# A fused linear layer with a low-rank term: unrolled programs over six tiles become loops over one ring, and chunks double in size

## The chip, the cores and the metric

The kernel runs on one core of a Trainium2 chip. The metric is device microseconds per execution. Three runs of the kernel before gave 165.13, 165.41 and 165.42 us, so the median is 165.41 us. All times inside an execution come from one profiled execution, counted from its first instruction.

## The reference

`x` has 16 × 2048 = 32768 rows of 256 float32 values. `W` is 256 × 256; the low-rank factors have rank 16.

```python
y = x_flat @ W
lora_out = x_flat @ lora_A
lora_out = lora_out * lora_E
lora_out = lora_out @ lora_B
y = y + scale * lora_out
```

The input is 33.5 MB, the output is as large, and the weights are small. Since everything is linear, the kernel builds one effective weight `weff = W + scale * A diag(E) B` once and multiplies every row by it.

## The kernel before, in words

**Chunks.** The rows are cut into nine chunks by `PLAN`, in units of 128 rows: 16, seven times 32, and 16. Below, "a 32-row chunk" means 32 rows on each of the 128 partitions, 4 MB; in memory each partition's share is one contiguous piece of 32 KB (16 KB for the short chunks). A chunk is loaded into one of six tiles `xy`, worked on in place, and stored from the same tile. Chunks 6, 7 and 8 reuse the tiles of chunks 0, 1 and 2.

**Steps.** A step is four rows per partition (`Q = 4`), so a 32-row chunk has 8 steps and the whole kernel 64. In a step VectorE (DVE) casts four rows to bf16 into `xb` (L146); TensorE (PE) makes eight 128×128 transposes of them into PSUM tile `ps_xt` (L176); DVE copies these to `xt` (L155); PE makes eight products with `weff` into `ps_y` (L184); ScalarE (ACT) copies the result over the input rows in `xy` (L163). `xb`, `xt`, `ps_xt` and `ps_y` have two buffers each.

**Order on the engines.** The order is written out by hand, with semaphores. DVE and ACT have all 64 steps unrolled. DVE casts step k+1 before it copies the transposes of step k. PE runs a loop of two steps with its work shifted by one step: it transposes step k+1 before it multiplies step k, so that the DVE copy of step k lies beside transposes of k+1. PE waits with `take`, an instruction that waits for a semaphore and lowers it by one (L170); DVE and ACT have their waits attached to the work instruction.

**Transfers.** All big transfers are issued by SyncE (SP) on one queue, which its 16 DMA engines work off in order. SP issues W and the loads of chunks 0 to 5 at once (L104, L102), then for each chunk waits until ACT has finished it (`s_rdy`, an ACT drain per chunk) and issues its store (L109). After the store of chunk 2 it issues the loads of chunks 6, 7 and 8, each after a wait until the store of the tile's former chunk has landed (`s_out`).

Of the kernel before, what the change touches and what calls it, by code (L numbers as in the profile page):

```python
# [6 lines left out]

PLAN = [16] + [32] * 7 + [16]  # L10

ROWS, SLOTS = 32, 6

LEAD = 6
AFTER = {2: [6, 7, 8]}

Q = 4


@with_exitstack  # L20
def kernel(
    ctx: ExitStack,
    tc: tile.TileContext,
    x: bass.AP,
    W: bass.AP,
    lora_A: bass.AP,
    lora_B: bass.AP,
    lora_E: bass.AP,
    scale: bass.AP,
    out: bass.AP,  # L30
):
    nc = tc.nc
    P = 128
    FP32 = mybir.dt.float32
    BF16 = mybir.dt.bfloat16

    x_flat = x.flatten_outer_dims()
    out_flat = out.flatten_outer_dims()
    N, K = x_flat.shape
    M = out_flat.shape[1]  # L40
    R = lora_B.shape[0]
    KC = K // P
    CHUNKS = len(PLAN)
    assert K == M and sum(PLAN) * P == N and all(b % Q == 0 for b in PLAN)

    def sbuf(name, shape, dt):
        return ctx.enter_context(nc.sbuf_tensor(name, shape, dt))

    def psum(name, shape, dt):
        return ctx.enter_context(nc.psum_tensor(name, shape, dt))  # L50

    xy = [sbuf(f"xy{s}", [P, ROWS, K], FP32) for s in range(SLOTS)]
    xb = [sbuf(f"xb{s}", [P, Q, K], BF16) for s in range(2)]
    xt = [sbuf(f"xt{s}", [P, Q, KC, P], BF16) for s in range(2)]
    w_sb = sbuf("w_sb", [P, KC, M], FP32)
    a_sb = sbuf("a_sb", [P, KC, R], FP32)
    b_sb = sbuf("b_sb", [R, M], FP32)
    e_sb = sbuf("e_sb", [R, 1], FP32)
    b_bf = sbuf("b_bf", [R, M], BF16)
    ate = sbuf("ate", [R, KC, P], BF16)  # L60
    weff = sbuf("weff", [P, KC, M], BF16)
    ident = sbuf("ident", [P, P], FP32)
    ident_bf = sbuf("ident_bf", [P, P], BF16)

    ps_xt = [psum(f"ps_xt{s}", [P, Q, KC, P], BF16) for s in range(2)]
    ps_y = [psum(f"ps_y{s}", [P, Q, M], FP32) for s in range(2)]
    ps_at = psum("ps_at", [P, KC, P], FP32)
    ps_aeb = psum("ps_aeb", [P, KC, M], FP32)

    sem = tc.alloc_semaphore  # L70
    s_w, s_a, s_b, s_e = sem("s_w"), sem("s_a"), sem("s_b"), sem("s_e")
    s_in = [sem(f"s_in{i}") for i in range(CHUNKS)]

    again = CHUNKS - SLOTS
    s_out = [sem(f"s_out{i}") for i in range(again + 1)]
    s_id = sem("s_id")
    s_lora = sem("s_lora")
    s_lpe = sem("s_lpe")
    s_xb = sem("s_xb")
    s_t = sem("s_t")  # L80
    s_xt = sem("s_xt")
    s_p = sem("s_p")
    s_y = sem("s_y")
    s_rdy = sem("s_rdy")

    starts = [sum(PLAN[:i]) * P for i in range(CHUNKS)]

    def rows_of(flat, i):
        b, r0 = PLAN[i], starts[i]
        return flat[r0:r0 + b * P, :].rearrange("(p b) k -> p b k", b=b)  # L90


    steps = [(i, r) for i, b in enumerate(PLAN) for r in range(0, b, Q)]
    n = len(steps)
    assert n % 2 == 0

    with tc.tile_critical(sync_engine=mybir.EngineType.SP, no_gpsimd_drain=True):  # L97
        sp, pe, dve, act, pool = nc.sync, nc.tensor, nc.vector, nc.scalar, nc.gpsimd


        def load(i):
            sp.dma_start(out=xy[i % SLOTS][:, :PLAN[i], :], in_=rows_of(x_flat, i)).then_inc(s_in[i], 16)  # L102

        sp.dma_start(out=w_sb[:], in_=W.rearrange("(c p) m -> p c m", p=P)).then_inc(s_w, 16)  # L104
        for i in range(LEAD):
            load(i)
        for i in range(CHUNKS):
            sp.wait_ge(s_rdy, i + 1)
            sp.dma_start(out=rows_of(out_flat, i), in_=xy[i % SLOTS][:, :PLAN[i], :]).then_inc(s_out[min(i, again)], 16)  # L109
            for later in AFTER.get(i, []):  # L110
                if later >= SLOTS:
                    sp.wait_ge(s_out[later - SLOTS], 16)
                load(later)
        for i in range(len(s_out) - 1):
            sp.wait_ge(s_out[i], 16)


        pool.memset(ident[:], 0.0).then_inc(s_id, 1)  # L118
        pool.wait_ge(s_id, 1)
        pool.affine_select(  # L120
            out=ident[:], in_=ident[:], compare_op=mybir.AluOpType.not_equal, fill=1.0,
            base=0, pattern=[[-1, P]], channel_multiplier=1,
        ).then_inc(s_id, 1)


        dve.wait_ge(s_id, 2)
        dve.tensor_copy(out=ident_bf[:], in_=ident[:]).then_inc(s_lora, 1)  # L127
        dve.wait_ge(s_b, 16)
        dve.tensor_copy(out=b_bf[:], in_=b_sb[:]).then_inc(s_lora, 1)  # L129
        dve.wait_ge(s_e, 16)  # L130
        dve.wait_ge(s_lpe, 1)
        dve.tensor_scalar(  # L132
            out=ate[:], in0=ps_at[:R, :, :], scalar1=e_sb[:], scalar2=float(scale),
            op0=mybir.AluOpType.mult, op1=mybir.AluOpType.mult,
        ).then_inc(s_lora, 1)
        dve.wait_ge(s_w, 16)
        dve.wait_ge(s_lpe, 2)
        dve.tensor_add(out=weff[:], in0=w_sb[:], in1=ps_aeb[:]).then_inc(s_lora, 1)  # L138

        def round_step(k):  # L140
            i, r = steps[k]
            if r == 0:
                dve.wait_ge(s_in[i], 16)
            if k >= 2:
                dve.wait_ge(s_t, k - 1)
            dve.tensor_copy(out=xb[k % 2][:], in_=xy[i % SLOTS][:, r:r + Q, :]).then_inc(s_xb, 1)  # L146

        round_step(0)
        for k in range(n):
            if k + 1 < n:  # L150
                round_step(k + 1)
            dve.wait_ge(s_t, k + 1)
            if k >= 2:
                dve.wait_ge(s_p, k - 1)
            dve.tensor_copy(out=xt[k % 2][:], in_=ps_xt[k % 2][:]).then_inc(s_xt, 1)  # L155


        act.dma_start(out=a_sb[:], in_=lora_A.rearrange("(c p) r -> p c r", p=P)).then_inc(s_a, 16)
        act.dma_start(out=b_sb[:], in_=lora_B).then_inc(s_b, 16)
        act.dma_start(out=e_sb[:], in_=lora_E[:, None]).then_inc(s_e, 16)  # L160
        for k, (i, r) in enumerate(steps):
            act.wait_ge(s_p, k + 1)
            act.copy(out=xy[i % SLOTS][:, r:r + Q, :], in_=ps_y[k % 2][:]).then_inc(s_y, 1)  # L163
            if r + Q == PLAN[i]:
                act.drain().then_inc(s_rdy, 1)

        def take(s):
            pe.wait_ge(s, 1).then_inc(s, -1)  # L170

        def transposes(k):
            take(s_xb)
            for j in range(Q):
                for c in range(KC):
                    t = pe.transpose(ps_xt[k % 2][:, j, c, :], xb[k % 2][:, j, c * P:(c + 1) * P], ident_bf[:])  # L176
            t.then_inc(s_t, 1)

        def products(k):
            take(s_xt)  # L180
            take(s_y)
            for j in range(Q):
                for c in range(KC):
                    m = pe.matmul(  # L184
                        ps_y[k % 2][:, j, :], xt[k % 2][:, j, c, :], weff[:, c, :],
                        start=(c == 0), stop=(c == KC - 1),
                    )
            m.then_inc(s_p, 1)

        pe.sem_inc(s_y, 2)  # L190
        pe.wait_ge(s_a, 16)
        pe.wait_ge(s_id, 2)
        for c in range(KC):
            t = pe.transpose(ps_at[:R, c, :], a_sb[:, c, :], ident[:])  # L194
        t.then_inc(s_lpe, 1)
        pe.wait_ge(s_lora, 3)
        for c in range(KC):
            m = pe.matmul(ps_aeb[:, c, :], ate[:, c, :], b_bf[:], start=True, stop=True)  # L198
        m.then_inc(s_lpe, 1)
        transposes(0)  # L200
        pe.wait_ge(s_lora, 4)
        with pe.Fori(0, n // 2 - 1):
            transposes(1)
            products(0)
            transposes(0)
            products(1)
        transposes(1)
        products(0)
        products(1)


    with tc.tile_critical(sync_engine=mybir.EngineType.SP, no_gpsimd_drain=True):
        nc.sync.wait_ge(s_out[again], 16 * (CHUNKS - again))
# [34 lines left out]
```

## Time and profile before

| | |
|---|---|
| median of three runs | 165.41 us |
| profiled execution | 165.19 us |
| its span, first to last instruction | 163.4 us |
| busy: PE, DVE, ACT | 90.8, 84.1, 66.1 us |
| moved by DMA | 67.43 MB, mean 413 GB/s |
| mean granted TensorE clock | 0.831 |

The profile counts an engine as busy while its instructions run. A group of instructions is shown with its line, engine, operation, the tiles written and read, the count, the busy time, the mean duration of one and the idle time in front of it, with what ended that idle time. "SPq" is SyncE's sequencer, which issues the transfers; a wait there is the time during which the next transfer was not yet put into the queue. The row "DMA" gives the busy share of the 16 DMA engines in 40 equal slices of 4.1 us, in tenths.

### The profile page before, as it was taken

The page shows a single profiled execution, that of the slowest core. Times are in us where ns is not written, and L with a number is a line of the kernel's source. Part 1 is how long each engine was busy: PE and PEld are TensorE (multiplying, and loading weights), DVE is VectorE, ACT ScalarE, POOL GpSimd, SP SyncE. Part 2 cuts the span into 40 slices and gives each one's busy share as a digit, 9 for nine tenths or more (in the row PEclk, how much of TensorE's full clock was granted, in tenths as well). Part 3 has the DMA queues.
Part 4 walks back from the last instruction along what each step waited for, and adds up shares of the span by engine and source line. Part 5 has one row for each costly group of instructions (what it writes and reads, how often), then busy time and mean ns, then how long its engine had stood idle before and what let it go on. Part 6 is the DMA issues. An engine that isn't in the chain of part 4 may idle for free. (4 is left out here: it accounts for less than half of the span.)

```text
span 163.4 us, 2684 instructions
## 1 busy us (share of the span) xinstructions
PE 90.8 (56%) x1028; PEld 81.6 (50%) x1028; DVE 84.1 (51%) x132; ACT 66.1 (40%) x65; POOL 0.7 (0%) x6
## 2 busy tenths in 40 slices
PE   0169499999999999990000099999992000000000
PEld 0047389999999999980000089999981000000000
DVE  0165299999999999950000169999970000000000
ACT  3002447777777777772000026777774000000000
POOL 1000000000000000000000000000000000000000
PEclk9999999999999999999555559999999755555555
DMA  4999999899999999999999998999999999999990
GB/s 133 421 433 489 393 449 449 385 473 425 403 481 393 385 409 481 393 457 425 433 433 425 441 441 383 465 437 425 425 435 433 441 409 465 417 425 441 409 409 32
DMA packets 3203, 67.43 MB, mean 413 GB/s; under 512 B 624, under 2 KB 896, under 8 KB 896
## 3 DMA queue, kind: packets, MB, share of 16 engines
q1 hardware_dynamic: 2864, 67.37, 96.4%
q10 hardware_dynamic: 336, 0.03, 0.3%
q14 instruction: 3, 0.02, 0.0%
HBM read 33.85 MB, written 33.55 MB: 412 GB/s over the span
## 5 line engine op out<-in xcount | busy, mean ns | idle before, releaser
L163 ACT COPY xy<-ps_y 128x1024 f32<-128x1024 f32 x64 | 64.8, 1013 | 56.2 <-PE ps_y L184 56.2
L184 PE MATMUL ps_y<-weff,xt 128*128 128x256 bf16 x512 | 68.6, 278 | 0.5 <-PEq L170 0.3
L146 DVE CAST xb<-xy 128x1024 bf16<-128x1024 f32 x64 | 43.6, 683 | 24.9 <-DMA xy<-in_x_dram 24.9
L176 PE MATMUL ps_xt<-ident_bf,xb 128*128 128x128 bf16 x512 | 40.9, 226 | 24.7 <-PEq L170 24.7
L184 PEld LDWEIGHTS ps_y<-weff,xt 128*128 128x128 bf16 x512 | 48.4, 100 | 6.4 <-issue 1.1
L176 PEld LDWEIGHTS ps_xt<-ident_bf,xb 128*128 128x128 bf16 x512 | 35.5, 102 | 27.3 <-issue 25.7
L155 DVE COPY xt<-ps_xt 128x1024 bf16<-128x1024 bf16 x64 | 44.2, 691 | 5.4 <-PE ps_xt L176 3.7
L194 PE MATMUL ps_at<-ident,a_sb 128*16 128x128 f32 x2 | 0.6, 402 | 4.1 <-DMA a_sb<-in_lora_A_dram 4.1
L198 PE MATMUL ps_aeb<-b_bf,ate 16*128 16x256 bf16 x2 | 0.6, 404 | 3.6 <-DVE ate L132 3.6
L129 DVE CAST b_bf<-b_sb 16x256 bf16<-16x256 f32 x1 | 0.3, 280 | 3.9 <-DMA b_sb<-in_lora_B_dram 3.9
L163 ACT ACT_TABLE_LOAD x1 | 1.3, 1283 | 2.5 <-issue 2.5
L198 PEld LDWEIGHTS ps_aeb<-b_bf,ate 16*128 16x128 bf16 x2 | 0.1, 106 | 4.1 <-DVE ate L132 4.1
L194 PEld LDWEIGHTS ps_at<-ident,a_sb 128*16 128x16 f32 x2 | 0.1, 94 | 4.1 <-DMA a_sb<-in_lora_A_dram 4.1
L132 DVE TENSOR_SCALAR ate<-ps_at,e_sb 16x256 bf16<-16x256 f32 x1 | 0.5, 472 | 1.6 <-DMA e_sb<-in_lora_E_dram 1.6
L127 DVE CAST ident_bf<-ident 128x128 bf16<-128x128 f32 x1 | 0.2, 227 | 1.7 <-POOL ident L120 1.7
L138 DVE TENSOR_TENSOR weff<-w_sb,ps_aeb 128x512 bf16<-128x512 f32 x1 | 0.7, 687 | 0.8 <-PE ps_aeb L198 0.8
L120 POOL TENSOR_SCALAR_AFFINE_SELECT ident<-ident 128x128 f32<-128x128 f32 x1 | 0.3, 293 | 0.2 <-POOL ident L118 0.2
L118 POOL MEMSET ident<- 128x128 f32 x1 | 0.2, 204 | 0.5 <-SPq L97 0.5
L229 POOL MEMSET const-bfloat16-1.0<- 128x1 bf16 x1 | 0.1, 101 | 0.0
L229 POOL MEMSET const-uint8-127<- 128x1 uint8 x1 | 0.1, 101 | 0.0
L229 POOL MEMSET const-float32-0.0<- 128x1 f32 x1 | 0.1, 98 | 0.2 <-issue 0.2
L229 POOL MEMSET const-float32-1.0<- 128x1 f32 x1 | 0.1, 98 | 0.0
## 6 DMA issues: line engine op xcount, KB each, us to landing
xy<-in_x_dram SPq DMA_DIRECT2D x7, 4096.0 KB, 29.1
out_dram<-xy SPq DMA_DIRECT2D x7, 4096.0 KB, 39.5
xy<-in_x_dram SPq DMA_DIRECT2D x2, 2048.0 KB, 16.3
out_dram<-xy SPq DMA_DIRECT2D x2, 2048.0 KB, 39.3
w_sb<-in_W_dram SPq DMA_DIRECT2D x1, 256.0 KB, 2.9
a_sb<-in_lora_A_dram ACTq DMA_DIRECT2D x1, 16.0 KB, 3.1
b_sb<-in_lora_B_dram ACTq DMA_DIRECT2D x1, 16.0 KB, 4.4
e_sb<-in_lora_E_dram ACTq DMA_DIRECT2D x1, 0.1 KB, 5.7
```

Of the source, the lines that this page charges most:

```text
L120: pool.affine_select(out=ident[:], in_=ident[:], compare_op=mybir.AluOpType.not_equal, fill=1.0, base=0, pattern=[[-1, P]], channel_multip ...
L129: dve.tensor_copy(out=b_bf[:], in_=b_sb[:]).then_inc(s_lora, 1)
L132: dve.tensor_scalar(out=ate[:], in0=ps_at[:R, :, :], scalar1=e_sb[:], scalar2=float(scale), op0=mybir.AluOpType.mult, op1=mybir.AluOpType. ...
L138: dve.tensor_add(out=weff[:], in0=w_sb[:], in1=ps_aeb[:]).then_inc(s_lora, 1)
L146: dve.tensor_copy(out=xb[k % 2][:], in_=xy[i % SLOTS][:, r:r + Q, :]).then_inc(s_xb, 1)
L155: dve.tensor_copy(out=xt[k % 2][:], in_=ps_xt[k % 2][:]).then_inc(s_xt, 1)
L163: act.copy(out=xy[i % SLOTS][:, r:r + Q, :], in_=ps_y[k % 2][:]).then_inc(s_y, 1)
L176: t = pe.transpose(ps_xt[k % 2][:, j, c, :], xb[k % 2][:, j, c * P:(c + 1) * P], ident_bf[:])
L184: m = pe.matmul(ps_y[k % 2][:, j, :], xt[k % 2][:, j, c, :], weff[:, c, :], start=(c == 0), stop=(c == KC - 1),)
L194: t = pe.transpose(ps_at[:R, c, :], a_sb[:, c, :], ident[:])
L198: m = pe.matmul(ps_aeb[:, c, :], ate[:, c, :], b_bf[:], start=True, stop=True)
L229: nc = _bacc.Bacc("TRN2", target_bir_lowering=False, num_devices=1)
```

## The change

`PLAN` becomes three chunks of 64 rows (8 MB, pieces of 64 KB) and two of 32. The six tiles become one tile `xy` of 192 rows, used as a ring: chunks 0, 1 and 2 fill it, and chunks 3 and 4 go into the two halves of chunk 0's place. SP issues three loads at the start, then the stores of chunks 0 and 1, and then, once store 0 has landed, the loads of chunks 3 and 4, and the remaining stores.

DVE and ACT no longer have unrolled programs but two loops each, a first pass over the ring of 24 turns and a second of 8. A turn is eight rows per partition, two steps. The address of a turn's rows in the ring is computed from the loop's counter. PE's loop now has 32 turns, and the shift by one step is gone: in a turn it transposes both steps and then multiplies both. DVE makes both casts and then both copies. The waits on DVE and ACT become `take` instructions. ACT drains and raises `s_rdy` in every turn. GpSimd (POOL) waits for each load and raises the semaphore `s_ld` by the number of turns that it holds; DVE takes one per turn.

In the built program each DVE and ACT loop body has an instruction for register arithmetic in front of each copy that uses the ring's address. In the body of ACT's first loop there also stands, between the first such instruction and the first copy, the load of the activation table; in the program before it stands once, ahead of the 64 copies. In ACT's second loop there is none.

```diff
-PLAN = [16] + [32] * 7 + [16]
-ROWS, SLOTS = 32, 6
-LEAD = 6
-AFTER = {2: [6, 7, 8]}
+PLAN = [64, 64, 64, 32, 32]
+RING = 192
+LEAD = 3
+AFTER = {1: [3, 4]}
 Q = 4
+TURN = 2 * Q
...
-    xy = [sbuf(f"xy{s}", [P, ROWS, K], FP32) for s in range(SLOTS)]
+    xy = sbuf("xy", [P, RING, K], FP32)
+    xy_turns = xy[:].rearrange("p (t k q) d -> p t k (q d)", k=2, q=Q)
...
         for i in range(CHUNKS):
-            sp.wait_ge(s_rdy, i + 1)
-            sp.dma_start(out=rows_of(out_flat, i), in_=xy[i % SLOTS][:, :PLAN[i], :]).then_inc(s_out[min(i, again)], 16)
+            sp.wait_ge(s_rdy, (starts[i] + PLAN[i]) // TURN)
+            sp.dma_start(out=rows_of(out_flat, i), in_=ring_of(i)).then_inc(s_out[min(i, again)], 16)
             for later in AFTER.get(i, []):
-                if later >= SLOTS:
-                    sp.wait_ge(s_out[later - SLOTS], 16)
+                sp.wait_ge(s_out[owner[later]], 16)
                 load(later)
...
+        for i in range(CHUNKS):
+            pool.wait_ge(s_in[i], 16).then_inc(s_ld, PLAN[i] // TURN)
...
-        round_step(0)
-        for k in range(n):
-            if k + 1 < n:
-                round_step(k + 1)
-            dve.wait_ge(s_t, k + 1)
-            if k >= 2:
-                dve.wait_ge(s_p, k - 1)
-            dve.tensor_copy(out=xt[k % 2][:], in_=ps_xt[k % 2][:]).then_inc(s_xt, 1)
+        for rows in passes:
+            with dve.Fori(0, rows // TURN) as turn:
+                take(dve, s_ld)
+                for k in range(2):
+                    dve.tensor_copy(out=xb[k][:], in_=xy_turns[:, bass.ds(turn, 1), k, :]).then_inc(s_xb, 1)
+                for k in range(2):
+                    take(dve, s_t)
+                    dve.tensor_copy(out=xt[k][:], in_=ps_xt[k][:]).then_inc(s_xt, 1)
...
-        for k, (i, r) in enumerate(steps):
-            act.wait_ge(s_p, k + 1)
-            act.copy(out=xy[i % SLOTS][:, r:r + Q, :], in_=ps_y[k % 2][:]).then_inc(s_y, 1)
-            if r + Q == PLAN[i]:
+        for rows in passes:
+            with act.Fori(0, rows // TURN) as turn:
+                for k in range(2):
+                    take(act, s_p)
+                    act.copy(out=xy_turns[:, bass.ds(turn, 1), k, :], in_=ps_y[k][:]).then_inc(s_y, 1)
                 act.drain().then_inc(s_rdy, 1)
...
-        transposes(0)
         pe.wait_ge(s_lora, 4)
-        with pe.Fori(0, n // 2 - 1):
+        with pe.Fori(0, turns):
+            transposes(0)
             transposes(1)
             products(0)
-            transposes(0)
             products(1)
-        transposes(1)
-        products(0)
-        products(1)
```

## The prediction

> **What bounds the kernel now.** I read the page's slices first, then the queue table, then the waits of SP.
>
> ```profile
> DMA  4999999899999999999999998999999999999990
> ...
> q1 hardware_dynamic: 2864, 67.37, 96.4%
> ...
> q14 instruction: 3, 0.02, 0.0%
> ```
>
> The DMA engines are full from the second slice to the last but one, and one queue carries nearly all of it. PE, DVE and ACT are busy for 56, 51 and 40% of the span. The transfers set the end, and compute counts only where it holds back a transfer. Next, where SP's queue waited, and how the chunks come through it:
>
> ```profile
> SPq L109 <- ACTq L165: 77.6, 7, 18.4
> SPq L102 <- DMA out_dram<-xy: 38.5, 3, 19.8
> SPq L243 <- DMA out_dram<-xy: 36.2, 1, 36.2
> ```
>
> ```profile
> 64.30 0.34 SPq L102 DMA_DIRECT2D xy<-in_x_dram  x1
> ```
>
> ```profile
> 73.99 0.34 SPq L102 DMA_DIRECT2D xy<-in_x_dram  x1
> ```
>
> ```profile
> 83.67 0.33 SPq L102 DMA_DIRECT2D xy<-in_x_dram  x1
> ```
>
> Loads 6, 7 and 8 go out when stores 0, 1 and 2 have landed; the distance of two landings, 9.68 us, is the time of 4 MB. SP waited for ACT 77.6 us in all without one idle DMA slice, since six loads (58 us) lay in the queue. The last store was issued long before its turn: the end is a 36.2 us wait for the queue. The third view is one compute step, warm (19 to 22 us) and after an idle spell (93 to 97 us):
>
> ```profile
> 19.26 0.69 DVE L146 CAST xb<-xy 128x1024 bf16<-128x1024 f32 x1 [3.37 <-DMA xy<-in_x_dram]
> ...
> 20.10 0.61 PE L176 MATMUL ps_xt<-ident_bf,xb 128*128 128x128 bf16 x8 [2.34 <-PEq L170]
> ...
> 20.85 1.03 PE L184 MATMUL ps_y<-weff,xt 128*128 128x256 bf16 x8
> ```
>
> ```profile
> 94.22 1.01 PE L176 MATMUL ps_xt<-ident_bf,xb 128*128 128x128 bf16 x8 [20.86 <-PEq L170]
> ...
> 95.03 1.91 PE L184 MATMUL ps_y<-weff,xt 128*128 128x256 bf16 x8
> ```
>
> ```profile
> L163 ACT COPY xy<-ps_y 128x1024 f32<-128x1024 f32 x64 | 64.8, 1013 | 56.2 <-PE ps_y L184 56.2
> ...
> L163 ACT ACT_TABLE_LOAD x1 | 1.3, 1283 | 2.5 <-issue 2.5
> ```
>
> Steady ACT copies start 1.32 us apart: 2.64 us for two steps, PE's own pace (0.45 us of transposes and 0.87 us of products a step, without a gap).
>
> **What the new order demands.** The bytes are the same. The packet records show 1213 ns for 32 KB and 611 ns for 16 KB, so a larger piece saves some 6 ns; a 64-row chunk takes 19.3 us, and all chunks 6 × 19.3 + 4 × 9.68 = 154.7 us against 155.0 us before. That is 0.3 us. The first chunk's packets began at 3.2 to 3.6 us, but most engines got their second only at 4.4 to 4.9 us; the first 64 KB packet (2.4 us) covers this: another 0.5 us. So load 0 lands at 22.9, load 1 at 42.2, load 2 at 61.6 us, and store 0 ends at 80.9. A spell of slow packets at 54.6 to 57.5 us cost each engine about 0.6 us; I keep it: 81.5 us. Then the queue is empty unless store 1 is in it. Behind store 1 in SP's program stand loads 3 and 4 (their wait for store 0 is over by then) and all other stores. W was issued at 0.94 us and its first packet ran at 2.03, so SP must issue store 1 by 80.4 us: 16 turns of compute have to be done by then. Before, this cover was six small loads; now it is three loads and one store.
>
> **When compute starts.** Before, data landed at 9.15 us and the first cast ran at 9.57: 0.4 us. POOL's relay (nothing is queued behind its five waits) and the address instruction add 0.2 to 0.3 (estimate from 0.05 to 0.15 us per semaphore instruction in the records). First cast 23.6; PE 0.84 us later (93.38 to 94.22) at 24.4. PE is cold: transposes 1.06, DVE's `take` 0.1, copy 0.69, PE's two takes 0.30 (20.55 to 20.85), products 1.9. The first `ps_y` is ready 4.1 us later, at 28.5 us.
>
> **A turn on PE and DVE.** Without the shift, products wait for this turn's copy: transposes 0.61, `take` 0.10, copy 0.69, takes 0.30, two lots of products 1.74: 3.44 us in place of 2.64. DVE needs 4 × 0.60 us plus its loop's branch and arithmetic, which run while the last copy runs; 0.8 us of slack cover them.
>
> **A turn on ACT.** Here is the largest term. The built program has the table load inside the first loop's body, behind the wait for `ps_y`, so I expect 24 of them in place of 1. ACT cannot overlap its turns either, as the drain holds its program until the second copy is written. So: table load 1.28, copies 0.92 and 1.01 (an estimate: DVE's operations overlap by 0.08 us when they touch; no two ACT copies of this trace do), and drain end, loop arithmetic, branch, `take`, address arithmetic. ACT shows none of these in a loop; PE's loop instruction and branch take 0.28 us, a `take` 0.08 to 0.15, an unconditional branch on SP or ACT about 0.15. I take 0.5 us for all; bounds 0.25 and 0.9, the ends of those rows for five instructions. Sum 3.75 us (3.5 to 4.15), more than PE's 3.44: ACT sets the turn. PE's missing shift is then hidden behind ACT; without the table load it would be the bound. A load of the table that is already active could in principle cost nothing; the one row says 1283 ns and I take it, nothing being nearer. The Trainium skill's page "ScalarE: Activation LUTs", section "What ACT_TABLE_LOAD costs", speaks against the change more strongly: 1283 ns (as here) and a drain of about 1380 ns for every switch to another set. By it the turn would be 5.1 us and the time about 195 us; the trace has no drain at its one load and the set is not switched, so I leave it out.
>
> **Loops and instruction fetch.** Three instruction packets ran during the execution, 0.31 us each, and each held up one engine by up to 0.95 us. Shorter programs should need none in mid-run, but the stall below aligns the 16 engines anyway. The page "Runtime: NRT & Kernel Launch", section "Instruction fetch mechanics", warns that a taken branch outside the two resident pages forces a fetch; here PE's branch was taken 30 times and PE waited 0.3 us in all before L184 for its sequencer, so I add nothing.
>
> **The sum.** ACT ends turn 16 at 28.5 + 16 × 3.75 − 0.3 (arithmetic of a turn that never comes) = 88.2 us. SP issues store 1 at 88.3, the first packet runs at 89.4: the DMA engines stand for 89.4 − 81.5 = 7.9 us. From there on the queue has stores 1 to 4 and loads 3 and 4, 77.4 us, without another gap: store 2 is ready at about 118.5 and needed at 128, store 3 at 137.5 (needed 147), store 4 at 151.5 (needed 157). Spread of the 16 engines 0.3, one lagging engine 0.4 (before, two ended 1.6 us after the others; part of that was built up before the time where the stall aligns them). End of transfers 89.4 + 77.4 + 0.7 = 167.5 us. The span before ended 1.67 us after the last packet (161.73), and the execution took 165.19 − 163.4 = 1.79 us more than its span: 171.0 us, against 165.19 of the profiled execution before. The median was 0.2 us above that, less than I can resolve. Each 0.1 us of ACT's turn is 1.6 us: 3.5 to 4.15 give 167 to 177.
>
> **The rivals.** First, PE sets the turn, since the table load is not repeated or costs little. For it: copying needs no new table. Against it: the built program and the 1283 ns row. Turn 3.44; the cold start costs 1 to 2 us; turn 16 ends at 82.9, store 1 runs at 84.0, a stall of 2.5 us; end 84.0 + 77.4 + 0.7 + 3.46 = 165.6 us, between 164.8 and 167. The stall is paid for by the 0.8 us saved on packets and by the lag of the last engines, which it wipes out.
>
> Second, on the other side, faster: compute stays under the queue altogether. It decides at 80.4 us for turn 16, that is a turn of 3.29 us or less, 0.15 below my sum on PE and 0.45 below that on ACT: cheaper handovers, and no repeated load. Then no slice is empty, and the transfers end at 3.4 + 154.7 + 0.6 + 0.7 = 159.4: 162.9 us, 162.3 to 164.3.
>
> Third, much slower: ACT's arithmetic costs a microsecond instead of a tenth (turn 4.7, time 171.0 + 16 × 0.95 = 186 us), or PE never gets its full clock (cold turn 1.06 + 0.10 + 0.69 + 0.30 + 2 × 1.71 = 5.6, about 200 us). Against a cold PE: the clock stayed full in this trace through stretches of 3.4 us that were 55% and 72% busy (15.9 to 22.7 us), and a turn is 70 to 80% busy. Against slow arithmetic: no instruction of that kind in the records takes over 0.3 us.
>
> **How the numbers follow.** ACT with the table load 0.74, PE's chain 0.13, under the queue 0.07, much slower 0.06. From 165.2 to 176.0 the range takes in most of the first two. A measurement of this kernel can tell 0.2% from no change, 0.33 us. Faster: the second rival and a third of the first, 0.12; the same: 0.04; slower: 0.84.
>
> **What would show it.** Right: the row ACT_TABLE_LOAD with 24 instances near 1283 ns; ACT copies in pairs about 3.7 us apart; SP's store of chunk 1 near 88 us with a wait for ACT in front; one hole of some two slices in the DMA row after half of the span, and none before or after. A single table load, or ACT waiting for PE in every turn, makes the first rival right; no hole at all the second. Two holes, or a low granted clock between 30 and 115 us, the third.

## The result, and the profile after

The changed kernel takes 175.11 us (median of 4 runs, 174.59 to 175.47) against 165.32 us of the kernel before in 4 runs: 1.059 times as long, with a 95% interval of 1.056 to 1.062. The profiled execution took 175.18 us with a span of 173.4 us. Forecast was 171.0 us in a range of 165.2 to 176.0: a loss of 5.8 us, where 9.8 were measured.

First the slices of the page of the kernel after. The transfers are interrupted once:

```profile
PEclk9999999999999999999999999998599999975555
DMA  8979995999959999595059799598999989999890
GB/s 306 397 333 484 484 484 242 484 484 484 484 242 484 484 484 469 257 484 242 0 242 408 317 484 484 242 484 363 484 363 484 454 348 408 408 431 469 386 469 15
```

A slice is 4.3 us. The 5s before the middle, with 242 GB/s, are no gaps: a 64 KB packet lasts 2.4 us and is put into slices as a whole, and the packet records run there without a break. The hole is `242 0 242` in the middle, two slices in all. There is no second one, and the granted clock is full for the first 27 slices, up to 117 us. Next, the groups of ACT and the waits of SP's queue (total, times, longest), both of the kernel after:

```profile
L175 ACT COPY xy<-ps_y 128x1024 f32 x64 | 61.8, 1015 | 18.2 <-ACTq L139 17.9
...
L175 ACT ACT_TABLE_LOAD x24 | 30.8, 1283 | 42.2 <-ACTq L139 42.2
```

```profile
SPq L121 <- ACTq L176: 147.3, 5, 56.6
SPq L246 <- DMA out_dram<-xy: 18.0, 1, 18.0
```

24 table loads of 1283 ns stand where one stood. SP now waits for ACT 147.3 us in place of 77.6, and its last wait for the queue is 18.0 us in place of 36.2: the last store is issued with half of the former backlog in front of it. The timeline of ACT around the hole (start, duration, what ran, and the idle time before it) gives the turn:

```profile
82.49 1.28 ACT L175 ACT_TABLE_LOAD   x1 [0.54 <-ACTq L139]
83.79 1.93 ACT L175 COPY xy<-ps_y 128x1024 f32 x2
86.25 1.28 ACT L175 ACT_TABLE_LOAD   x1 [0.53 <-ACTq L139]
87.54 1.93 ACT L175 COPY xy<-ps_y 128x1024 f32 x2
90.00 1.28 ACT L175 ACT_TABLE_LOAD   x1 [0.54 <-ACTq L139]
```

A turn is 3.755 us: load 1.28, two copies 1.93, and 0.54 us in which ACT drains, does its loop's arithmetic, branches and takes its semaphore. PE in the same stretch shows who waits for whom:

```profile
82.97 1.06 PE L183 MATMUL ps_xt<-ident_bf,xb 128*128 128x128 bf16 x16
84.94 1.95 PE L191 MATMUL ps_y<-weff,xt 128*128 128x256 bf16 x16 [0.92 <-PEq L139]
```

PE stands for 0.92 us before its products. It takes there the signal of DVE's copy and that of ACT's copy, which frees the buffer of `ps_y`, and ACT's is the later one: ACT's first copy of the turn ends at 84.80 us, DVE's first at 84.42. SP's own timeline has the moment that matters. A row that covers several issues runs from the start of the first to the end of the last, so the store of chunk 1 ends the first row:

```profile
59.48 30.39 SPq L121 DMA_DIRECT2D out_dram<-xy  x2
89.92 1.41 SPq L114 DMA_DIRECT2D xy<-in_x_dram  x2
119.58 33.80 SPq L121 DMA_DIRECT2D out_dram<-xy  x3
```

By the instruction records it was issued at 89.53 us. The packet records show store 0 ending at 81.1 to 81.4 us on 15 of the 16 DMA engines and at 82.7 on one, and the first packets of store 1 at 90.37 to 90.52: those 15 stood for 9.0 to 9.4 us.

### The profile page after: what moved, and what is told of

Read it like the earlier page. It is cut to its first block, busy times and chain, and to the rows that moved or that the text cites. A ratio compares the mean times of both kernels' runs of the same rounds, so it can differ in the third digit from the quotient of the medians.

```text
span 173.4 us, 3142 instructions
## 1 busy us (share of the span) xinstructions
PE 96.5 (56%) x1028; PEld 80.5 (46%) x1028; DVE 81.8 (47%) x132; ACT 92.6 (53%) x88; POOL 0.7 (0%) x6
## 5 line engine op out<-in xcount | busy, mean ns | idle before, releaser
L191 PE MATMUL ps_y<-weff,xt 128*128 128x256 bf16 x512 | 64.6, 279 | 26.2 <-PEq L139 25.5
L175 ACT COPY xy<-ps_y 128x1024 f32 x64 | 61.8, 1015 | 18.2 <-ACTq L139 17.9
L191 PEld LDWEIGHTS ps_y<-weff,xt 128*128 128x128 bf16 x512 | 47.5, 99 | 39.9 <-issue 31.0
L165 DVE COPY xt<-ps_xt 128x1024 bf16<-128x1024 bf16 x64 | 41.4, 687 | 39.6 <-DVEq L139 39.6
L175 ACT ACT_TABLE_LOAD x24 | 30.8, 1283 | 42.2 <-ACTq L139 42.2
L162 DVE CAST xb<-xy 128x1024 bf16 x64 | 41.2, 685 | 14.3 <-DVEq L139 14.3
L183 PE MATMUL ps_xt<-ident_bf,xb 128*128 128x128 bf16 x512 | 35.6, 225 | 14.9 <-PEq L139 14.9
L183 PEld LDWEIGHTS ps_xt<-ident_bf,xb 128*128 128x128 bf16 x512 | 32.8, 101 | 16.4 <-issue 15.6
```

Of the source, the lines that this page charges most:

```text
L162: dve.tensor_copy(out=xb[k][:], in_=xy_turns[:, bass.ds(turn, 1), k, :]).then_inc(s_xb, 1)
L165: dve.tensor_copy(out=xt[k][:], in_=ps_xt[k][:]).then_inc(s_xt, 1)
L175: act.copy(out=xy_turns[:, bass.ds(turn, 1), k, :], in_=ps_y[k][:]).then_inc(s_y, 1)
L183: t = pe.transpose(ps_xt[k][:, j, c, :], xb[k][:, j, c * P:(c + 1) * P], ident_bf[:])
L191: m = pe.matmul(ps_y[k][:, j, :], xt[k][:, j, c, :], weff[:, c, :], start=(c == 0), stop=(c == KC - 1),)
```

## The experiments

The theory is the prediction's: the repeated table load makes ACT's turn 3.75 us, store 1 comes too late for the queue, and the transfers never make up the hole. The rivals are that the loss belongs to the chunks or to the loops themselves, whatever ACT does. Times are medians, and ratios are to the kernel before in the same session. All kernels start from the kernel after, and diffs are against it.

### The table load once

```diff
+    warm = sbuf("warm", [R, 1], FP32)
...
+        act.wait_ge(s_b, 16)
+        act.copy(out=warm[:], in_=b_sb[:, 0:1])
         for rows in passes:
             with act.Fori(0, rows // TURN) as turn:
```

> The changed kernel with one tiny ScalarE copy ahead of the loops, so that the table load stands there once and not in the loop. Theory (ScalarE's turn with a table load in it makes store 1 late): 1 table load in place of 24, the turn falls from 3.76 to about 3.49 us, which is what the second pass shows, store 1 is issued near 84 us in place of 89.5, and the time falls by the same 5.3 us to 168 to 170 us. A stall of 3 to 4 us is left, which belongs to the missing shift of TensorE. Rival (TensorE and VectorE without the shift set the turn anyway, and the table load lies in their shade): no change, 175 us. Rival (the stall has another cause, such as 8 MB transfers): no change either.

169.39 us, 1.024 [1.019, 1.029]. Lines of its groups, its slices and ACT's timeline:

```profile
L173 ACT ACT_TABLE_LOAD x1 | 1.3, 1283 | 2.5 <-issue 2.5
```

```profile
DMA  8699979979995996999199599989897999799990
```

```profile
78.07 1.93 ACT L178 COPY xy<-ps_y 128x1024 f32 x2 [1.57 <-ACTq L140]
81.56 1.93 ACT L178 COPY xy<-ps_y 128x1024 f32 x2 [1.56 <-ACTq L140]
```

One early copy draws the load out of the loop. The turn falls to 3.49 us, now set by the PE and DVE chain (ACT idles 1.56 us in it); store 1 goes out at 83.55, and the hole shrinks to one slice, all as the theory said. The place of the load in the loop is worth 5.7 us of the loss of 9.8 (175.11 less 169.39; 5.8 by the two ratios).

### The chunks and the ring alone

DVE and ACT are unrolled and PE has its shift by one step, as in the kernel before; `PLAN`, ring, `LEAD` and `AFTER` are those of the kernel after.

```diff
-        for rows in passes:
-            with dve.Fori(0, rows // TURN) as turn:
...
+        round_step(0)
+        for k in range(n):
+            if k + 1 < n:
+                round_step(k + 1)
...
+        for k, (i, r) in enumerate(steps):
+            act.wait_ge(s_p, k + 1)
+            act.copy(out=ring_of(i, r, Q), in_=ps_y[k % 2][:]).then_inc(s_y, 1)
```

> The ring, the plan and the transfers of the changed kernel with the unrolled programs and the shifted TensorE loop of the kernel before. Theory: a turn of two steps is 2.64 us, store 1 is ready near 70 us, the queue never runs dry, and the time is 164 to 165.5 us, a little under the kernel before, since the pieces are larger. Rival (the large chunks themselves cost the time, by the late start of compute or by slower packets): 168 us or more, with a hole in the DMA row.

165.97 us, 1.002 [1.001, 1.003]: level with the kernel before, and above what was expected. Store 1 was issued at 70.89 us; the slices have no hole, and the row for instruction packets has the three of the kernel before:

```profile
DMA  8699899959959989899989969999999996999960
...
q14 instruction: 3, 0.02, 0.0%
```

So the chunks alone do not lose the 9.8 us. They do not gain either, though 14 of its 16 engines ended at 159.64 us or sooner, 0.4 us ahead of the same 14 before. Two came at 161.71 and 162.38. The packet records tell them apart. The one at 161.71 stood for 0.30 us beside two of the three instruction packets (at 54.33 and 134.38 us), and its packets right behind them took 0.64 and 0.41 us too long; the rest of its lag is from one spell near 60 us. The one at 162.38 has 64 KB packets that are 0.2 us too long in its stores beside compute; the later experiments deal with this one.

### The loops alone, with small chunks

```diff
-PLAN = [64, 64, 64, 32, 32]
+PLAN = [32] * 8
...
-LEAD = 3
-AFTER = {1: [3, 4]}
+LEAD = 6
+AFTER = {2: [6], 3: [7]}
```

> The loops and the ring of the changed kernel, table load in the loop included, with eight chunks of 32 rows, six of them loaded at the start. Theory: the slow turn of 3.76 us stays, but store 0 and store 1 are ready at some 34 and 49 us, long before the queue needs them (61 and 71 us), so no hole appears and the time is that of the kernel before, 164.5 to 166.5 us. Rival (slow turns cost wherever they stand): 24 turns with 1.1 us more each show in the end, 172 us or more.

167.41 us, 1.011 [1.008, 1.014]. The 24 table loads and the turn of 3.755 us are all there, and no slice is empty:

```profile
L175 ACT ACT_TABLE_LOAD x24 | 30.8, 1283 | 31.8 <-ACTq L139 31.8
```

```profile
DMA  5999999989999899999999999999999999899940
```

So the slow turn costs nearly eight microseconds less where six small loads cover it. The rest was not expected: 15 engines ended by 159.80 us and one at 163.66. The end of the kernel hung on one DMA engine of 16, 3.9 us behind.

### Small chunks first

```diff
-PLAN = [64, 64, 64, 32, 32]
+PLAN = [32, 32, 64, 64, 32, 32]
...
-LEAD = 3
-AFTER = {1: [3, 4]}
+LEAD = 4
+AFTER = {2: [4, 5]}
```

> The changed kernel with its first 64-row chunk split in two: 32, 32, 64, 64, 32, 32. Nothing else is changed, the table load stays in the loop. Theory: compute starts 9.7 us earlier, so turn 16 ends near 80 us, about when the queue needs that store (81 us): the hole of 9 us closes to 0 to 1 us, 164.5 to 167.5 us. Rival (the number or size of the queued transfers, not the start of compute, matters): still near 175 us.

167.47 us, 1.012 [1.008, 1.016], at the top of what was expected, again without a hole and with one engine late (163.61, the others by 159.61). The same ring and 64-row chunks with the slow loops lose 7.6 us less than after when compute can begin on 32 rows.

### Transfers alone

No step is computed; every chunk is stored as it was loaded.

```diff
-            sp.wait_ge(s_rdy, (starts[i] + PLAN[i]) // TURN)
+            sp.wait_ge(s_in[i], 16)
...
-        for rows in passes:
-            with dve.Fori(0, rows // TURN) as turn:
...
-        with pe.Fori(0, turns):
```

> The changed kernel with the 32 turns left out: every chunk is loaded and, when it has landed, stored as it came, in the same order on the same queue; the effective weight is still built. It shows what the transfers of this plan take alone. Theory (one of the 16 DMA engines is held up while stores run beside compute; in the kernel with loops alone it ended 4 us after the others): without compute all 16 end within 0.6 us of each other, 158.4 us plus one or two spells of slow packets, and the time is 162 to 164 us. Rival (the late engine belongs to the stores or to the chip): one engine is again 2 to 4 us late, 165 us or more.

163.16 us, 0.986 [0.983, 0.989], as expected. All engines end between 158.91 and 159.57 us. This is what these transfers take, and it has no late engine: compute makes it late.

### A quarter of PE's work

This is the kernel with the small chunks and the slow loops, but after its first turn PE does two of eight transposes and products in a step; nearly three quarters of the output are left out.

```diff
+        with pe.Fori(0, turns - 1):
+            transposes(0, Q - 1)
+            transposes(1, Q - 1)
+            products(0, Q - 1)
+            products(1, Q - 1)
```

> The kernel with loops alone (eight chunks of 32 rows), in which TensorE after its first turn does only the last two of the eight transposes and of the eight products of each step, so 16 of its 64 instructions per turn; three quarters of the product are left out. VectorE and ScalarE do all their work, and ScalarE's table load keeps the turn at 3.76 us, so every transfer is issued when it was. Theory A (the late DMA engine is held up by TensorE, by its reads or by its number of instructions): its lag at the end falls from 4 us to 1 to 1.8 us, and the time from 167.4 to 164.5 to 165.5. Theory B (it is held up by what VectorE and ScalarE read and write): the lag stays near 4 us and the time at 167.4 us.

165.88 us, 1.002 [1.000, 1.004]. ACT's turn stays at 3.76 us and the stores go out at the same times, so the pace of compute does not make the engine late. 1662 instructions are left of 3152, and the last engine ends at 161.78, 1.7 us after the fourteenth: a result between the two expectations, with about half of the lag for about half of the instructions. A second engine (161.48) was late as well, by 0.75 us since its first packets, 0.5 us from a spell near 60 us and 0.5 us from one packet at 100 us; why, is open.

### Loops with the shift and one table load

DVE casts the next turn's first step before it makes this turn's second copy, PE is shifted as before, and the early copy of the first experiment is kept. The last turn of each pass stands outside DVE's loop.

```diff
-        for rows in passes:
-            with dve.Fori(0, rows // TURN) as turn:
-                take(dve, s_ld)
-                for k in range(2):
...
+        def dve_turn(turn, after):
+            cast(turn, 1)
+            copy(0)
+            if after is not None:
                 take(dve, s_ld)
+                cast(after, 0)
+            copy(1)
+        take(dve, s_ld)
+        cast(0, 0)
+        for p, rows in enumerate(passes):
+            last = rows // TURN - 1
+            with dve.Fori(0, last) as turn:
+                dve_turn(turn, turn + 1)
+            dve_turn(last, 0 if p == 0 else None)
```

> The changed kernel with both faults of its turn mended, loops and chunks kept: the table load stands once ahead of the loops, and the work of TensorE and VectorE is shifted by one step again inside the loops (the last turn of each pass stands behind its loop). Theory: the turn is TensorE's own 2.64 us, store 1 is issued near 70 us, there is no hole, and the time is 164.5 to 166 us, that of the kernel with the new chunks alone; so loops as such cost nothing. Rival (branches, register arithmetic and takes cost time in every turn): turn of 3 us or more, and 166.5 us or more.

166.74 us, 1.006 [1.003, 1.009]. ACT's timeline and the slices:

```profile
59.20 2.10 ACT L192 COPY xy<-ps_y 128x1024 f32 x2 [0.55 <-ACTq L140]
61.84 2.10 ACT L192 COPY xy<-ps_y 128x1024 f32 x2 [0.55 <-ACTq L140]
```

```profile
DMA  8699979969997989979979996999999799999930
```

A turn of 2.64 us: loops and ring addresses cost compute nothing against the unrolled programs. Store 1 goes out at 71.91, no slice is empty, no instruction packet runs. Against the first experiment the shift is worth 2.65 us by the medians and 3.0 by the ratios. The time is above the 164.5 to 166 us of the theory and in the range of the rival, but not for the rival's reason, as the turn is not longer. What is left over the kernel before, 1.0 to 1.4 us, goes with a late engine: 163.78 us, the others by 159.94 (in an execution of 167.31 us, the longest of the five), where the kernel before has its last two at 161.65 and 161.73.

### What makes one engine late

Two kernels without `x`'s product separate the two candidates, the number of instructions and the data that compute moves. The first has the transfers alone, and loops on PE, DVE and ACT that raise and take a semaphore; the second has the transfers alone, and copies of one small tile on DVE and ACT with few instructions. Every chunk is stored as loaded.

```diff
+        def idle(name, engine, times):
+            with engine.Fori(0, times):
+                for _ in range(8):
+                    engine.sem_inc(s_idle[name], 1)
+                    take(engine, s_idle[name])
```

```diff
+        with dve.Fori(0, 60):
+            for _ in range(4):
+                dve.tensor_copy(out=xb[0][:, 0:KC, :], in_=w_sb[:]).then_inc(s_own["dve"], 1)
+                take(dve, s_own["dve"])
...
+        with act.Fori(0, 48):
+            for _ in range(4):
+                act.copy(out=xb[1][:, 0:KC, :], in_=ps_aeb[:]).then_inc(s_own["act"], 1)
+                take(act, s_own["act"])
```

> The transfers alone, beside which TensorE, VectorE and ScalarE each run a loop of nothing but semaphore instructions (raise by one, take one) for most of the execution, some 25 to 30 instructions per us in all, as the kernel with loops has; no data is read or written, and the chunks are stored as they came. Theory C (one DMA engine's stores are slowed by the number of instructions that the core executes, whatever they do): one engine ends 2 to 5 us after the others, which end within 0.7 us, and the time is 165 to 168 us. Rival D (it is slowed by what the engines read and write): all 16 end within 0.7 us, about 163 us.

> The transfers alone, beside which VectorE and ScalarE copy one small tile over and over (512 elements per partition, so that both are busy for most of the time) with about 7 instructions per us in place of 26; TensorE does nothing, and the chunks are stored as they came. Theory C: a lag of about a quarter of the 4 us of the kernel with loops, 0.7 to 1.5 us. Rival D: with both engines as busy as in that kernel or more, a lag of 2 to 4 us.

217.35 and 172.98 us in one run each. These times are the length of the loops, which outlast the transfers, and the total is not what the runs are read by. Read are the ends of the 16 engines, with the number of instructions in the trace (each engine's end is the completion packet of its share of the last store, in us, sorted):

```
kernel                            instructions    8th     14th    15th    16th
before                                    2684  159.48  160.08  161.65  161.73
chunks alone                              2667  159.38  159.64  161.71  162.38
loops alone, small chunks                 3152  159.58  159.78  159.80  163.66
small chunks first                        3146  159.38  159.58  159.61  163.61
loops shifted, one table load             3078  159.49  159.73  159.94  163.78
the kernel after                          3142  169.89  170.06  170.18  171.64
the table load once                       3120  163.85  164.13  164.14  165.61
a quarter of PE's work                    1662  159.52  160.11  161.48  161.78
transfers and empty instructions          4243  159.35  159.87  159.93  165.41
transfers and copies                      1186  159.62  159.88  160.47  161.37
transfers alone                            101  159.24  159.49  159.51  159.57
```

In the kernel after and in the one with the table load once the stall aligned the engines, and what one of them had lost by then does not show at the end. Empty instructions, which move no data, make one engine later (5.5 us, more than the 2 to 5 expected) than all of the real compute does; 104 us of copies on DVE and 114 on ACT, with few instructions, leave it 0.9 us behind the fifteenth and 1.5 behind the fourteenth.

The late engine's packets during stores, by the instructions that the trace shows per microsecond at that time, point the same way:

```
stretch of stores                         instructions per us   64 KB packet longer by
empty instructions, three engines                    28               250 ns
empty instructions, ACT's loop over                  16               137 ns
loops shifted                                        35               250 ns
chunks alone                                         30          193 to 221 ns
the table load once                                  27          160 to 193 ns
the kernel after, store of chunk 1                   25          147 to 208 ns
```

Among the kernels that compute, the excess grows with the number; an empty instruction weighs more than an average one of theirs. 32 KB packets show the same: the median of the lengthened ones is 42 ns too long at 13 instructions per us (a quarter of PE's work), 89 at 26 (loops alone), and about 100 at 31 (the kernel before, stores at 64 to 72 and 108 to 116 us). The first two of these kernels execute the same semaphore operations and differ in matmuls and weight loads alone, so it is not the semaphores by themselves. The 32 KB packets of the kernel with copies were mostly longer by 18 to 46 ns at 7 instructions per us. In loads the excess is near nothing: with the empty loops running the last engine was 3.20 us behind when store 1 ended, at 105.1 us, and 3.27 us behind when the two loads behind it had ended at 124.5. So the instructions that run beside a store set the lag, by their number and less by what they are. That theory holds, and the one of data traffic falls.

### Which engine it is

```diff
+        for k in range(1, 16):
+            sp.dma_start(out=mark[:k, 24 * k:25 * k + 8], in_=W[:k, :8 + k]).then_inc(s_mark, 16)
```

> The kernel with the shift inside its loops and one table load, and behind its last store 15 small loads: the k-th takes k rows of W, of 32 + 4 k bytes each, into a tile that nothing reads. They are there to number the 16 engines: a load of k rows is cut into k packets, and I expect that they go to the k lowest numbered engines (so says the Trainium skill, page 'DMA: Direct Memory Access', section 'Why a DMA increments its semaphore by 16 and not by 1'; no trace here has shown it yet). So the engine with number j should run the packets of the loads with k > j, behind its own last store packet, and the late engine is named by the sizes that come after the others are done. Theory that the lag belongs to one fixed engine: one engine ends at 163.5 to 164 us as in the kernel without these loads, the other 15 by 160.2, and the sizes that are late tell one number. Rival, that any engine can be the one and two or more share the lag here: packets of several patterns are late. The loads cost 15 x 50 to 100 ns at the end of the queue, so I expect 167 to 169.5 us, and nothing is read from that.

(The page's title is "DMA: Bandwidth & Descriptors"; the expectation has it wrong.) One run, 168.81 us. The packet records of the last 4 us, all of one engine, completion packets of 4 bytes left out:

```
start us   bytes          start us   bytes
159.260    32768          163.083    68
160.550    32768          163.097    72
161.816    32768          163.111    76
163.031    52             163.125    80
163.044    56             163.139    84
163.057    60             163.153    88
163.070    64             163.167    92
```

The record holds k packets of the size of load k, for every k. The other 15 engines had run all theirs by 159.30 us. The late engine has the packets of the loads with 5 to 15 rows and none of those with 1 to 4: by the page's rule it is engine number 4, counted from 0. That is one execution, and no run shows whether it is the same one in the other kernels. What links a store on that engine to instructions elsewhere stays open: the Trainium skill's page "NOTIFIC — the notification-queue block", in the paragraph under its title, tells of an instruction trace whose 16-byte records are written to rings in memory. No run here shows that such writes meet this engine. But every time here may have been taken with such a trace on, and then the lag could be one of the measurement.

None of these kernels that computes the whole result beats the kernel before: the nearest, the chunks alone, is level with it.

## Why the prediction was right

The direction and the mechanism held, and the time lay within its range, near the upper end. The loss itself was 1.7 times the forecast, mainly from terms behind the stall that were set too low. By its steps:

- **ACT's turn.** Predicted 3.75 us from 1.28 + 0.92 + 1.01 + 0.5; measured 3.755, with 0.54 for the last term. That the last one came out so near is partly luck: 0.5 was picked between bounds of 0.25 and 0.9. 24 table loads of 1283 ns, as predicted, although the table was active already. The Trainium skill's page "ScalarE: Activation LUTs", section "What ACT_TABLE_LOAD costs", was right on the 1283 ns; the drain that it adds for a switch to another set does not occur here, where the set stays the same: the copies start within 1.3 us of the load's start. Taking the load out gave back 5.7 us.
- **PE's turn.** Predicted 3.44 us; 3.49 where the load stood once. That PE's missing shift is hidden behind ACT, and is the bound without the load, was shown by the first and the seventh experiment.
- **Start of compute.** First cast at 24.13 in place of 23.6 (load 0 landed at up to 23.4, not 22.9), first table load at 29.19 in place of 28.5, and from the first to the second load ACT took 4.47 us, which the sum took as 3.75, since PE began slowly (its first 16 products took 3.57 us, later ones 1.95). Turn 16 was done, and store 1 issued, at 89.53 in place of 88.3. The Trainium skill's page "Runtime: NRT & Kernel Launch", section "Instruction fetch mechanics", warned of instruction fetches at taken branches; neither the kernel after nor the one with shifted loops shows an instruction packet in mid-run, and leaving them out was right.
- **The stall.** Predicted 7.9 us, measured 9.0 to 9.4: 1.2 from the later issue, 0.2 from store 0 ending before 81.5, less 0.25 since the first packet ran 0.85 us after the issue, not 1.1. The predicted spell of slow packets near 55 us was absent.
- **The queue after the stall.** Here are the terms that were mis-sized. Predicted were 77.4 us and 0.7 for spread and lag, from 89.4 to 167.5. The late engine ran from 90.52 to 171.65, 81.13 us. Its own packets add up to 77.3 us at their usual length. A spell of slow packets at 127.5 to 129.5 us adds 1.32 (it hit all 16; an earlier one at 105 to 109 us cost the other 15 engines 0.5 to 1.1 us and spared this one). The excess in stores 1 and 2 beside compute is 2.4, where 0.4 had been allowed for a lag: the prediction read the lag before as partly old and left behind by the stall. It is made anew in every store that runs beside instructions. Start +1.1, lag and spread +1.7, slow spell +1.3 come to the 4.1 us by which the profiled execution was over the forecast.
- **The tail.** 3.53 us from the last packet to the end of the execution, 3.46 predicted.
- **Slips of the sum.** 6 × 19.3 + 4 × 9.68 is 154.5 us and not 154.7, which makes the second rival's 162.9 us 0.2 too long, and by the packet rows a piece of 32 KB saves 9 ns against two of 16 KB and not 6. Neither bears on the 171.0 us.

**The rivals.** The first came about in the kernel with one table load: 169.4 us where it was priced at 165.6, with a turn as predicted. The second, compute under the queue, came about in the chunks alone and the shifted loops: no hole, as said, but 166.0 and 166.7 in place of 162.9. The first price was too low by 1.9 us of lag, by a spell of slow packets near 124 us that cost the late engine 1.2 us, and by a start 0.4 us later. The second was too low by the lag; 14 or 15 engines ended where it said (159.4 predicted, 159.6 to 159.9 measured). Its chance of a kernel faster than before was therefore too high. The third did not occur. The windows of the kernel after (stretch, its length, busy time of PE, weight loads, DVE, ACT and POOL, granted clock, DMA share, GB/s) show a full clock up to the stall:

```profile
24.00:90.00 66.00, 50.38 (x540) 42.21 (x541) 43.75 (x70) 51.37 (x48) 0.00 (x0) 1.00 0.85 365
```

Of the 9.8 us, the table load's place took 5.7 to 5.8 and the missing shift 2.65 to 3.0, taken out in this order; the shift with the load still in the loop was not run. The last 1.0 to 1.4 us, by difference, stay with everything under the queue. The shifted loops show one thing that costs there, an engine 3.8 us late; how much larger pieces and the absence of instruction packets give back was not measured apart.

## What to carry to other kernels

When programs become loops, look in the built program for what the compiler has put inside the body: a one-time step of 1.3 us became 24, and one tiny operation of the same kind ahead of the loop took it out. Count the cover in the queue in microseconds when chunks grow: the same slow turn cost a hole with three large loads in front and none with six small ones. Where transfers set the end, look at each DMA engine's own end and not only at the mean share: one engine of 16 decided the last 1.5 to 4 us here, and neither the row DMA nor the waits show it. Whether it is as late when no profile is taken, no run here shows.

## What was not expected of the hardware

- One DMA engine of 16 is slower by up to 10% during stores, the more instructions the compute engines run (250 ns per 64 KB at 28 per us, 137 ns at 16), even when these move no data. It is not slower in loads, and not without instructions.
- Each run had one to three spells in which most engines ran one or two packets slowly and lost 0.2 to 1.2 us on average, transfers alone included (0.64 us at 56 to 62 us). Mostly there was one, near 60 us; the kernel after had none there, but one near 108 and one near 129 us. What they are is open.
- A load of the activation table that is already active takes the full 1283 ns, each of 23 times.
